# A written-out issue order for 17 tiles of a ConvFFN, with sums of block products grown in PSUM

## The chip, the cores and the metric

The kernel runs on one core of a Trainium2 chip. The metric is the device time of one execution in microseconds (us), for the whole two-layer network. TensorE (PE) multiplies, VectorE (DVE), ScalarE (ACT) and GpSimd (POOL) do the rest, and SyncE (SP) issues the DMAs.

## The reference

Two trunk layers over 1024 latent tokens and 256 context tokens of width 1024: Fourier mixing and a gating MLP in layer 0, neighbourhood attention in layer 1, and behind each a ConvFFN with 2816 inner channels. The change concerns the ConvFFN of layer 1, which has the latent tokens alone:

```python
def conv_ffn(h, w_up, conv_w, conv_b, w_down):
    L = h.shape[1]
    a = h @ w_up
    gate, val = a[..., :D_FF], a[..., D_FF:]
    gp = jnp.pad(gate, ((0, 0), (CONV_W // 2, CONV_W // 2), (0, 0)))
    g = gp[:, 0:L] * conv_w[0] + gp[:, 1:1 + L] * conv_w[1] + gp[:, 2:2 + L] * conv_w[2] + conv_b
    return (jax.nn.silu(g) * val) @ w_down
...
        x = x + g2 * conv_ffn(modulate(x, norm2_g[layer], sh2, sc2),
                              ffn_w_up[layer], ffn_conv_w[layer], ffn_conv_b[layer], ffn_w_down[layer])
```

All of it is float32. `gate` and `val` come from one matrix `w_up` of 1024 x 5632.

## The kernel before

Every float32 operand of a matmul is held as two parts, a high one (a rounded copy, written by ScalarE) and a low one (the rest, `TENSOR_TENSOR` subtract, on VectorE or GpSimd). A product of two such operands is three matmuls (`PASSES`).

The tokens of a ConvFFN are worked in two halves (`s` = 0 and 1). A half has 2 x 256 columns in the first and 2 x 258 in the second (a few overlap for the convolution). Inside a half, a loop over `f` = 0 to 21 makes one tile of 128 gate and 128 value channels at a time (`up`, L274). With the channels split in gate and value, the inner dimension in two, and the columns in two, a tile is a 2 x 2 block product, done with seven products instead of eight:

- P1 = A00 B00, P2 = A01 B10, P3 = S4 B11, P4 = A11 N4, P5 = S1 T1, P6 = S2 T2, P7 = S3 T3, where A00, A01 come from the weights of the gate channels (load 0), A10, A11 from those of the value channels (load 1), and S1 = A10 + A11, S3 = A00 - A10, S2 = S1 - A00, S4 = A01 - S2.
- c00 = P1 + P2 is the gate for the first columns, c01 the gate for the second ones, c10 and c11 the values. They need U = P1 + P6 and V = U + P7: c01 = U + P5 + P3, c11 = V + P5, c10 = V + P4.

Each product is 12 matmuls of 128x256 (128x258 in the second half) into a PSUM bank of its own (`pq`, 8 banks). VectorE adds the products up in SBUF with seven sums (`add`, L311); ScalarE copies P1. Then follow the gate (L315, ScalarE: the middle tap and the bias), two taps on VectorE (L317, L319), silu (L321), the product with the values (L361), and the high and low part of the result, `act`.

The down projection of a pair of tiles is spread over the two tiles that come later: in tile f four down products D0 to D3 (`down`, L366; 6 matmuls of 128x512 each, or 12 of 128x258), each added to the residual stream by VectorE (L382, one row per D; X0 to X3 below).

Weights for tile f+1 are prepared in tile f (`up_weights`, L222). Two loads of 512 KB go through SP into the two buffers of `wr`; GpSimd makes S1 (L241), S3 (L247), S2 (L248) and S4 (L251) out of them, S3, S2 and S4 in place of what they were made from. Each of the seven A and S matrices is then split into a high part (ScalarE, L447) and a low part (L448). In tiles with down products, GpSimd makes the low parts of A00, A01 and A11 (`POOL`), VectorE those of the four sums. `wh` and `wq` hold the parts, one buffer for each matrix. The weights of the down projection (`wrd`, 512 KB for every tile, `wd` for the parts) are split on ScalarE and VectorE (`prep`).

The order in the program is made by a scheduler that works with an estimated timeline. The code gives it only the order of the products (`ORDER`), which steps of the weights follow which product (`FEED`), and how many down products follow one (`AFTER`); sums and the tail of a tile have high priority. Engines issue in the order that results, and wait for each other by semaphores.

Of the kernel before, what the change touches and what calls it, by code (L numbers as in the profile page):

```python
# [15 lines left out]
P = 128  # L16
# [62 lines left out]
class Ffn:  # L79
# [145 lines left out]
    def up_weights(self, f, slots):  # L225
# [27 lines left out]
        steps = {x: lambda x=x: split(x) for x in ("A00", "S2", "S1", "S4", "A01", "S3", "A11")}  # L253
        steps.update(load0=lambda: load(0), load1=lambda: load(1), s=rows)
# [19 lines left out]
    def up(self, s, f, hooks, downs, prep, beside):  # L274
# [4 lines left out]
        g0 = s * NF + f  # L279
        self.busy = len(downs) > 0  # L280
        if g0 == 0:
# [18 lines left out]

        def product(p):
            wn, bn = self.PROD[p]
            o = net.t(net.ps, [P, 512], "pq" if p in ("P2", "P5") else "pq")[:, :n]
            for k in range(4):
                for i, (wp, sp) in enumerate(PASSES):
                    nc.tensor.matmul(o, w[wn][:, wp, k], self.part(s, bn, k, sp), start=(k == 0 and i == 0),  # L306
                                     stop=(k == 3 and i == 2))
            return o

        def add(o, x, y):  # L310
            nc.vector.tensor_tensor(o, x, y, ALU.add)  # L311

        def gate():
            w0, w1, w2 = (cw[:, j * NF + f:j * NF + f + 1] for j in range(3))
            nc.scalar.activation(g, C0, AF.Identity, bias=net.convb[:, layer * NF + f:layer * NF + f + 1], scale=w1)  # L315
# [5 lines left out]
            nc.scalar.activation(g, g, AF.Silu)  # L321
        x = {}
        todo = [("P1", lambda: nc.scalar.activation(c00, x["P1"], AF.Copy)),
                ("P1 P6", lambda: add(c10, x["P6"], c00)),
# [5 lines left out]
                ("P6 P5 P3", lambda: add(c01, c01, x["P3"])),  # L330
                ("P6 P5 P3 P2", gate)]
        order, feed = (self.ORDER if f else self.ORDER0, self.FEED if f >= 2 - s else (self.FEED0, self.FEED1)[f])
        cut = 3 - f if f < 2 and s == 0 else 7
        for i, p in enumerate(order):
# [18 lines left out]
            for fn in downs[:m]:  # L353
                fn()
# [12 lines left out]

    def down(self, s, j, d, blocks=None):
        nc, net = self.nc, self.net
        fs = j // 2 * 2, j // 2 * 2 + 1  # L370
        h = self.halves[s]
        for lo, m in blocks or self.blocks(s):
# [5 lines left out]
            for st, t0, num, c in h.live:  # L378
                a, b = max(lo, c), min(lo + m, c + num)
                if a < b:  # L380
                    x = self.xs[st][d][:, t0 + a - c:t0 + b - c]
                    nc.vector.scalar_tensor_tensor(x, pd[:, a - lo:b - lo], net.mod[:, self.layer, st, 5, d:d + 1], x,  # L382
                                                   ALU.mult, ALU.add)

    def run(self, hooks, beside, early, done):


        def prep(j):
# [3 lines left out]
            if j < NF:  # L392
                self.fetch(j)
        for s, norm in ((0, self.ahead()), (1, beside)):
            if s == 1:
                next(beside, None)
            ups = []
            for f in range(NF):
                ups.append(self.up(s, f, hooks, [lambda d=d, j=f - 2: self.down(s, j, j % 2 * 4 + d) for d in range(4)]
                                   if 2 <= f < NF - 1 else [], lambda f=f: prep(f),  # L400
# [1393 lines left out]
```

## Time and profile before

| | us |
|---|---|
| median of 3 runs | 2921.48 (2912.1 to 2925.05) |
| the profiled execution | 2920.99 |
| its span in the profile | 2919.1 |
| layer 1's ConvFFN in it, from its first products to the end | about 2130 to 2919 |

The span is what the profile covers; 1.9 us of the execution lie around it. "Busy" of TensorE comes from modelled ends of pipelined matmuls. The granted clock of TensorE is given as a share of full speed. Where the chain of waits is quoted, each row is a piece of work that released the next.

### The profile page before, as it was taken

Reading aid. Unit: us, or ns where it says so; the run is one execution under the profiler, and the core shown is the slowest. Engines: PE = TensorE matmul, PEld = TensorE weight load, DVE = VectorE, ACT = ScalarE, POOL = GpSimd, SP = SyncE. Lnnn points to the kernel's source line nnn. Section 1 sums busy time; section 2 is a strip of 40 time slices with the busy share of each in tenths; the row PEclk is TensorE's granted clock in tenths of the full one; section 3 lists DMA queues with packets and bytes.
Section 4 is the critical chain, followed back from the end, with each engine's and each line's share of the span. In section 5 each row is a group of like instructions: output and inputs, shape, how many; then the busy total and the mean of one; then the engine's idle time right before and its main releaser. Section 6 shows DMA issues by size and latency. Waiting matters only on the chain.

```text
span 2919.1 us, 47590 instructions
## 1 busy us (share of the span) xinstructions
PE 2772.8 (95%) x17978; PEld 2522.4 (86%) x17978; DVE 2216.9 (76%) x3748; ACT 1302.0 (45%) x2448; POOL 1267.9 (43%) x1044
## 2 busy tenths in 40 slices
PE   7999998899999999999999998999989999899998
PEld 4668877799999899999888888998778888799998
DVE  4243477999989999998767668996498777887786
ACT  4221314434444443443443336996354444444443
POOL 0600025455555755553311112443455665666663
PEclk9999999899999999999899999999989999999999
DMA  8663262322223222222052327772133323333323
GB/s 303 215 189 118 98 217 72 112 74 86 80 87 101 75 80 87 73 81 87 24 169 101 137 109 183 180 179 80 37 109 101 95 87 98 105 89 93 94 88 95
DMA packets 335886, 327.67 MB, mean 112 GB/s; under 512 B 16217, under 2 KB 264617, under 8 KB 335657
## 3 DMA queue, kind: packets, MB, share of 16 engines
q1 hardware_dynamic: 331509, 315.69, 35.9%
q0 software_dynamic: 3808, 7.87, 0.9%
q8 instruction: 143, 2.34, 0.3%
q10 hardware_dynamic: 340, 1.06, 0.1%
q14 instruction: 86, 0.70, 0.1%
HBM read 277.86 MB, written 46.71 MB: 111 GB/s over the span
## 4 chain that ended last, share of the span: by engine, by line
PE 61%; DVE 14%; DMA 7%; POOL 7%; issue 5%; ACT 5%; SPq 0%; POOLq 0%; DVEq 0%; ACTq 0%
PE pq L306 18%; PE pq L478 15%; PE pq L376 11%; PE ps L478 6%; DMA wr<-in_ffn_w_up_dram 4%; POOL ws L241 2%; DVE xl L382 2%; DVE wh L448 2%; PE pq L566 2%; POOL wh L448 2%; DVE hx L311 2%; PE ps L487 2%; ACT t L1227 1%; POOL wr L248 1%; DMA wd<-in_ada_w_dram 1%
## 5 line engine op out<-in xcount | busy, mean ns | idle before, releaser
L376 PE MATMUL pq<-act,wd 128*128 128x320 f32 (+3 forms) x3696 | 639.8, 322 | 59.3 <-DVE xl L382 24.5
L376 PEld LDWEIGHTS pq<-act,wd 128*128 128x128 f32 x3696 | 557.1, 193 | 92.0 <-DVE xl L382 28.7
L306 PE MATMUL pq<-hs,wh 128*128 128x320 f32 (+3 forms) x4128 | 607.5, 299 | 16.3 <-DVE xl L382 7.8
L306 PEld LDWEIGHTS pq<-hs,wh 128*128 128x128 f32 x4128 | 576.9, 191 | 26.4 <-DVE xl L382 11.2
L306 PE MATMUL pq<-hs,wq 128*128 128x320 f32 (+3 forms) x3144 | 469.8, 299 | 8.4 <-DVE wq L448 4.9
L478 PE MATMUL pq<-hs,wh 128*128 128x512 f32 (+3 forms) x2100 | 469.0, 358 | 3.6 <-DVE hs L724 1.9
L306 PEld LDWEIGHTS pq<-hs,wq 128*128 128x128 f32 x3144 | 442.5, 191 | 14.1 <-DVE wq L448 5.7
L478 PEld LDWEIGHTS pq<-hs,wh 128*128 128x128 f32 x2100 | 365.8, 193 | 78.0 <-issue 6.2
L241 POOL TENSOR_TENSOR ws<-wr 128x512 f32<-128x512 f32 x88 | 153.6, 1745 | 397.3 <-DMA wr<-in_ffn_w_up_dram 333.0
L447 ACT ACTIVATE wh<-wr 128x512 fp32r<-128x512 f32 (+1 forms) x223 | 161.8, 726 | 354.0 <-POOL wr L248 201.5
L382 DVE SCALAR_TENSOR_TENSOR xl<-pq,mod,xl 128x320 f32<-128x320 f32 (+5 forms) x616 | 304.1, 514 | 11.7 <-PE pq L376 11.6
L448 DVE TENSOR_TENSOR wh<-wr,wh 128x512 fp32r<-128x512 f32 (+1 forms) x147 | 166.9, 1135 | 184.8 <-ACT wh L447 184.5
L448 POOL TENSOR_TENSOR wq<-wr,wq 128x512 fp32r<-128x512 f32 x152 | 235.7, 1550 | 32.9 <-ACT wq L447 32.9
L478 PE MATMUL ps<-hs,wh 128*128 128x512 f32 x840 | 240.0, 405 | 3.6 <-ACT hs L721 1.8
L311 DVE TENSOR_TENSOR hx<-hx,pq 128x320 f32<-128x320 f32 (+3 forms) x440 | 196.1, 448 | 29.1 <-PE pq L306 21.6
L447 ACT ACTIVATE wq<-wr 128x512 fp32r<-128x512 f32 x262 | 160.0, 623 | 101.3 <-PE pq L306 73.2
L447 ACT ACTIVATE wh<-ws 128x512 fp32r<-128x512 f32 x172 | 107.5, 625 | 169.8 <-PE pq L306 115.4
L478 PEld LDWEIGHTS ps<-hs,wh 128*128 128x128 f32 x840 | 141.9, 191 | 41.6 <-issue 14.4
L251 POOL TENSOR_TENSOR ws<-wr 128x512 f32<-128x512 f32 x88 | 120.2, 1366 | 123.3 <-DVE wh L448 112.3
L999 POOL TENSOR_TENSOR hsp<-hsq,hsp 128x512 fp32r<-128x512 f32 (+1 forms) x40 | 47.1, 1185 | 265.5 <-ACT hsq L998 265.5
L1006 DVE RECIPROCAL hsq<-hsq 128x512 f32<-128x512 f32 (+1 forms) x40 | 121.1, 3030 | 52.9 <-ACT hsq L1005 52.1
L448 DVE TENSOR_TENSOR wd<-wrd,wd 128x512 fp32r<-128x512 f32 x176 | 155.5, 912 | 0.2 <-ACT wd L447 0.2
(310 smaller groups left out, 4555.5 us busy)
## 6 DMA issues: line engine op xcount, KB each, us to landing
wr<-in_ffn_w_up_dram SPq DMA_DIRECT2D x176, 512.0 KB, 4.4
wrd<-in_ffn_w_down_dram SPq DMA_DIRECT2D x88, 512.0 KB, 3.5
adaw<-in_ada_w_dram SPq DMA_DIRECT2D x128, 256.0 KB, 3.6
wd<-in_ada_w_dram SPq DMA_DIRECT2D x32, 512.0 KB, 5.1
wr<-in_odd_w_qkv_dram SPq DMA_DIRECT2D x24, 512.0 KB, 3.9
vd<-kvs SPq DMA_DIRECT2D x8, 1280.0 KB
v<-vd SPq DMA_DIRECT2D x16, 640.0 KB
kd<-kvs SPq DMA_DIRECT2D x8, 1280.0 KB, 4.6
```

Of the source, the lines that this page charges most:

```text
L241: op(raw["S1"], raw["A10"], raw["A11"], ALU.add)
L251: op(x, raw["A01"], raw["S2"], ALU.subtract)
L306: nc.tensor.matmul(o, w[wn][:, wp, k], self.part(s, bn, k, sp), start=(k == 0 and i == 0), stop=(k == 3 and i == 2))
L311: nc.vector.tensor_tensor(o, x, y, ALU.add)
L376: nc.tensor.matmul(pd, self.wds[j][i][:, wp, d % 4], self.acts[f][:, sp, lo:lo + m], start=(i == 0 and pi == 0), stop=(i == len(fs) - 1 an ...
L382: nc.vector.scalar_tensor_tensor(x, pd[:, a - lo:b - lo], net.mod[:, self.layer, st, 5, d:d + 1], x, ALU.mult, ALU.add)
L447: self.nc.scalar.activation(h, src, AF.Copy)
L448: return (e or self.nc.vector).tensor_tensor(l, src, f32(h), ALU.subtract)
L478: nc.tensor.matmul(o, w(wp, k), s(k, sp), start=(ki == 0 and pi == 0), stop=(ki == len(order) - 1 and pi == 2))
L487: nc.tensor.matmul(out, l[a], r[b], start=(first and i == 0), stop=(last and i == 2))
L566: nc.tensor.matmul(acc[32 * q:32 * q + 32, 0:256], self.sT[:, k, :], w[q // 2][:, 256 * (q % 2):256 * (q % 2) + 256], start=(k == 0), stop ...
L1006: nc.vector.reciprocal(r, r)
```

## The change

For layer 1 alone, tiles 4 to 20 of each half get an issue order that is written out as a list (`STEADY`), and the scheduler leaves PE, DVE, ACT and POOL in it; SP's issues are still placed by it. Other tiles and layer 0 keep their code. In the list P1 to P7 are products, D0 to D3 down products and X0 to X3 their additions, h and l the high and low parts, c00 to c11 with U and V the copies and sums, s the sum S1; a name with a minus belongs to the tile before.

In these tiles
- P6 grows on the PSUM bank of P1, P7 on that and P4 on that; P3 grows on the bank of P5. ScalarE copies P1, U, V and V + P4 out; VectorE is left with three sums (c00+, c11+, c01+).
- all seven low parts of the up weights are made by VectorE; GpSimd makes the four sums.
- high and low part of a matrix are separate steps. So are the two loads, the gate and its taps, and a down product and its addition. X2, X3, silu, the product with the values and the parts of `act` are issued in the next tile; the down products follow P7, P4 and P3, and the down weights are split behind P1.

```diff
@@ class Ffn
+    STEADY = ("P1", "X2-", "prep", "P2", "c00", "silu-", "mul-", "hA00", "P6", "acth-", "c00+", "actl-", "P5", "U", "hA01",
+              "lA00", "X3-", "P7", "hS1", "lS1", "D0", "V", "c11+", "lA01", "P4", "hS2", "hS3", "X0", "lS2", "D1", "c10",
+              "lS3", "load0", "hA11", "P3", "lA11", "load1", "X1", "D2", "hS4", "c01+", "gate", "lS4", "taps", "D3", "s")
+    FIRST, LAST = 4, NF - 2
@@ up_weights
-        def split(name):
+        def high(name):
+            nc.scalar.activation(slots[name][:, 0], raw[name], AF.Copy)
+
+        def low(name):
             x = raw[name]
-            net.split(slots[name][:, 0], slots[name][:, 1], x, nc.gpsimd if self.busy and name in self.POOL else None)
+            e = nc.gpsimd if self.busy and name in self.POOL else nc.vector
+            e.tensor_tensor(slots[name][:, 1], x, f32(slots[name][:, 0]), ALU.subtract)
             if name == "A00":
                 op(raw["A10"], x, raw["A10"], ALU.subtract)
                 op(x, raw["S1"], x, ALU.subtract)
...
@@ up
-        self.busy = len(downs) > 0
...
+        steady = self.layer == 1 and self.FIRST <= f <= self.LAST
+        self.busy = len(downs) > 0 and not steady
+        bank, adds = {}, {}
 
-        def product(p):
+        def product(p, onto=None):
+
             wn, bn = self.PROD[p]
-            o = net.t(net.ps, [P, 512], "pq" if p in ("P2", "P5") else "pq")[:, :n]
+            o = net.t(net.ps, [P, 512], "pq")[:, :n] if onto is None else onto
             for k in range(4):
                 for i, (wp, sp) in enumerate(PASSES):
-                    nc.tensor.matmul(o, w[wn][:, wp, k], self.part(s, bn, k, sp), start=(k == 0 and i == 0),
-                                     stop=(k == 3 and i == 2))
+                    nc.tensor.matmul(o, w[wn][:, wp, k], self.part(s, bn, k, sp),
+                                     start=(onto is None and k == 0 and i == 0), stop=(k == 3 and i == 2),
+                                     skip_group_check=onto is not None)
             return o
...
+        if steady:
+
+            onto = dict(P6="P1", P7="P6", P4="P7", P3="P5")
+            ops = {"c00": lambda: copy(c00, x["P1"]), "c00+": lambda: add(c00, c00, x["P2"]),
+                   "U": lambda: copy(c01, x["P6"]), "V": lambda: copy(c10, x["P7"]),
+                   "c11+": lambda: add(c11, c10, x["P5"]), "c10": lambda: copy(c10, x["P4"]),
+                   "c01+": lambda: add(c01, c01, x["P3"]), "gate": gate, "taps": taps, "prep": prep}
+            for tok in self.STEADY:
+                if tok in self.PROD:
+                    x[tok] = product(tok, x[onto[tok]] if tok in onto else None)
+                elif tok[0] == "D":
+                    adds["X" + tok[1]] = downs[int(tok[1])](True)
+                elif tok[-1] == "-":
+                    if tok[:-1] in before:
+                        before[tok[:-1]]()
...
+            self.before = dict(after, **adds)
+            return
...
@@ run
+                if f == Ffn.FIRST and self.layer == 1:
+                    region = self.net.tc.manual_schedule(engines={engines.PE, engines.DVE, engines.Activation, engines.Pool})
+                    region.__enter__()
+                if f == Ffn.LAST + 1 and self.layer == 1:
+                    region.__exit__(None, None, None)
```


Below are rows of the program in its order, one tile of the first half. First GpSimd, before: `wr_23812` is load 0, `wr_23840` load 1, `ws` holds S1 and then S4, `wh` and `wq` the parts.

```order
L241 TENSOR_TENSOR ws_23878<-wr_23840 128x512
L247 TENSOR_TENSOR wr_23840<-wr_23812,wr_23840 128x512
L448 TENSOR_TENSOR wh_20746<-wr_23812,wh_20746 128x512
L248 TENSOR_TENSOR wr_23812<-ws_23878,wr_23812 128x512
L448 TENSOR_TENSOR wq_20648<-wr_23812,wq_20648 128x512
L251 TENSOR_TENSOR ws_23878<-wr_23812 128x512
L448 TENSOR_TENSOR wq_20973<-wr_23840,wq_20973 128x512
```

The same in the changed kernel (loads `wr_23773` and `wr_23789`), with the first row of the next tile:

```order
L248 TENSOR_TENSOR ws_23812<-wr_23789 128x512
L258 TENSOR_TENSOR wr_23789<-wr_23773,wr_23789 128x512
L259 TENSOR_TENSOR wr_23773<-ws_23812,wr_23773 128x512
L262 TENSOR_TENSOR ws_23812<-wr_23773 128x512
L248 TENSOR_TENSOR ws_23979<-wr_23956 128x512
```

The three low parts (L448) have left GpSimd; the four sums follow each other.

ScalarE before, from the copy of P1 to the next gate:

```order
L323 ACTIVATE hx_23884<-pq_23886 128x256
L321 ACTIVATE g_23713<-g_23713 128x512
L447 ACTIVATE wq_20648<-wr_23812 128x512
L447 ACTIVATE act_23880<-g_23713 128x512
L447 ACTIVATE wh_20746<-wr_23812 128x512
L447 ACTIVATE wh_20747<-ws_23878 128x512
L447 ACTIVATE wq_20649<-wr_23840 128x512
L447 ACTIVATE wq_20973<-wr_23840 128x512
L447 ACTIVATE wh_20747<-ws_23878 128x512
L315 ACTIVATE g_23885<-hx_23884,cols_31_139,cols_175_786 128x512
```

ScalarE in the changed kernel, from the copy of P1 to the high part of A11:

```order
L332 ACTIVATE hx_23814<-pq_23816 128x256
L353 ACTIVATE g_23648<-g_23648 128x512
L251 ACTIVATE wh_20746<-wr_23773 128x512
L348 ACTIVATE act_23867<-g_23648 128x512
L332 ACTIVATE hx_23814<-pq_23816 128x256
L251 ACTIVATE wq_20648<-wr_23773 128x512
L251 ACTIVATE wh_20747<-ws_23812 128x512
L332 ACTIVATE hx_23814<-pq_23816 128x256
L251 ACTIVATE wh_20746<-wr_23773 128x512
L251 ACTIVATE wq_20649<-wr_23789 128x512
L332 ACTIVATE hx_23814<-pq_23816 128x256
L251 ACTIVATE wq_20973<-wr_23789 128x512
```

All four copies (L332) read one bank, `pq_23816`, and stand among the high parts in the places that the list gives them; the silu of the tile before (L353) now stands behind the copy of P1, and the high part of `act` (L348) ahead of U's copy.

VectorE before, from the product with the values:

```order
L361 TENSOR_TENSOR g_23885<-g_23885,hx_23884 128x512
L311 TENSOR_TENSOR hx_24056<-pq_24089,hx_24056 128x256
L448 TENSOR_TENSOR act_24052<-g_23885,act_24052 128x512
L311 TENSOR_TENSOR hx_24056<-hx_24056,pq_24072 128x256
L448 TENSOR_TENSOR wh_20746<-wr_23984,wh_20746 128x512
L311 TENSOR_TENSOR hx_24056<-pq_24114,hx_24056 128x256
L448 TENSOR_TENSOR wh_20747<-ws_24050,wh_20747 128x512
L311 TENSOR_TENSOR hx_24056<-hx_24056,pq_24138 128x256
L311 TENSOR_TENSOR hx_24056<-hx_24056,pq_24114 128x256
L448 TENSOR_TENSOR wq_20649<-wr_24012,wq_20649 128x512
L382 SCALAR_TENSOR_TENSOR xl_2932<-pq_24128,mod_127,xl_2932 128x510
L311 TENSOR_TENSOR hx_24056<-hx_24056,pq_24158 128x256
```

VectorE in the changed kernel, from the same product of the tile before:

```order
L354 TENSOR_TENSOR g_23815<-g_23815,hx_23814 128x512
L329 TENSOR_TENSOR hx_23981<-hx_23981,pq_24005 128x256
L352 TENSOR_TENSOR act_24034<-g_23815,act_24034 128x512
L256 TENSOR_TENSOR wh_20746<-wr_23940,wh_20746 128x512
L449 SCALAR_TENSOR_TENSOR xl_3793<-pq_23972,mod_127,xl_3793 128x510
L256 TENSOR_TENSOR wh_20747<-ws_23979,wh_20747 128x512
L329 TENSOR_TENSOR hx_23981<-hx_23981,pq_24038 128x256
L256 TENSOR_TENSOR wq_20648<-wr_23940,wq_20648 128x512
L449 SCALAR_TENSOR_TENSOR xl_2932<-pq_24072,mod_127,xl_2932 128x510
L256 TENSOR_TENSOR wh_20746<-wr_23940,wh_20746 128x512
L256 TENSOR_TENSOR wq_20649<-wr_23956,wq_20649 128x512
L256 TENSOR_TENSOR wq_20973<-wr_23956,wq_20973 128x512
```

Of the sums (L311 before, L329 now) two of this stretch are left, low parts (L256) of A00, A01 and A11 have come in, and the first addition of a down product there, X3, belongs to the tile before.

## Rows read from the trace of the kernel before

**Rows 1.** The page: the span, and busy time by engine (share, instructions).
```profile
span 2919.1 us, 47590 instructions
...
PE 2772.8 (95%) x17978; PEld 2522.4 (86%) x17978; DVE 2216.9 (76%) x3748; ACT 1302.0 (45%) x2448; POOL 1267.9 (43%) x1044
```
**Rows 2.** Stretches (us): length, busy time of PE, PEld, DVE, ACT, POOL; clock; DMA share, GB/s.
```profile
1090.00:1360.00 270.00, 269.87 (x1808) 267.77 (x1807) 246.93 (x422) 111.01 (x180) 148.71 (x98) 1.00 0.27 79
2190.42:2479.18 288.76, 272.95 (x1848) 251.07 (x1847) 225.10 (x360) 123.93 (x220) 175.88 (x119) 0.98 0.32 94
2576.57:2877.74 301.17, 278.01 (x2233) 274.98 (x2232) 231.47 (x427) 125.87 (x223) 195.54 (x121) 0.98 0.30 90
2376.85:2392.37 15.52, 15.52 (x110) 14.45 (x110) 12.06 (x20) 7.26 (x13) 9.39 (x7) 1.00 0.27 84
2594.41:2610.29 15.88, 15.88 (x134) 15.88 (x133) 11.95 (x22) 6.81 (x13) 9.94 (x7) 1.00 0.35 101
```
**Rows 3.** Timeline of ScalarE: gates of tiles 3 and 20, first half (start, us).
```profile
2190.42 0.82 ACT L315 ACTIVATE g<-hx,cols,cols 128x512 f32<-128x512 f32 x1 [1.38 <-DVE hx L311]
...
2479.18 0.82 ACT L315 ACTIVATE g<-hx,cols,cols 128x512 f32<-128x512 f32 x1 [1.96 <-DVE hx L311]
```
**Rows 4.** Chain of waits, one period of the first half: start, us, what.
```profile
2240.36 4.92 DMA wr<-in_ffn_w_up_dram
...
2245.41 1.33 POOL ws L241
...
2246.82 1.62 POOL wr L247
2248.45 1.70 POOL wh L448
...
2250.22 1.30 POOL wr L248
...
2251.55 0.64 ACT wh L447
...
2252.22 1.10 DVE wh L448
...
2254.41 1.29 POOL ws L251
2255.70 1.76 POOL wq L448
...
2257.48 4.62 DMA wr<-in_ffn_w_up_dram
```
**Rows 5.** Groups by line, 2200 to 2480 us: busy us, mean ns | idle before.
```profile
L382 DVE SCALAR_TENSOR_TENSOR xl<-pq,mod,xl 128x510 f32<-128x510 f32 x67 | 49.5, 740 | 0.0
L311 DVE TENSOR_TENSOR hx<-hx,pq 128x256 f32<-128x256 f32 x83 | 34.0, 410 | 0.6
...
L448 DVE TENSOR_TENSOR wh<-ws,wh 128x512 fp32r<-128x512 f32 x33 | 23.6, 715 | 0.0
...
L447 ACT ACTIVATE wh<-ws 128x512 fp32r<-128x512 f32 x33 | 20.6, 625 | 31.8 <-POOL ws L251 28.5 <-PE pq L306 2.8 <-POOL ws L241 0.5
...
L317 DVE SCALAR_TENSOR_TENSOR g<-hx,cols,g 128x511 f32<-128x511 f32 x16 | 11.9, 741 | 0.0
...
L323 ACT ACTIVATE hx<-pq 128x256 f32<-128x256 f32 x16 | 5.8, 364 | 0.0
```
**Rows 6.** Timeline, all engines, near 2331 us: start, us, engine, what.
```profile
2330.32 1.83 POOL L241 TENSOR_TENSOR ws<-wr 128x512 f32<-128x512 f32 x1 [5.04 <-DMA wr<-in_ffn_w_up_dram]
...
2330.93 0.42 DVE L311 TENSOR_TENSOR hx<-pq,hx 128x256 f32<-128x256 f32 x1
...
2331.71 0.98 DVE L448 TENSOR_TENSOR act<-g,act 128x512 fp32r<-128x512 f32 x1 [0.37 <-ACT act L447]
```
**Rows 7.** Chain of waits, a tile without waits: products (48) and one down product (6).
```profile
2376.85 5.69 PE pq L306 x48
2382.54 1.38 PE pq L376 x6
```

More of the change, by code (lines that the diff above doesn't have):

```diff
@@ L252, in split @@
                 raw["S4"] = x
-        steps = {x: lambda x=x: split(x) for x in ("A00", "S2", "S1", "S4", "A01", "S3", "A11")}
+        steps = {}
+        for x in ("A00", "S2", "S1", "S4", "A01", "S3", "A11"):
+            steps.update({"h" + x: lambda x=x: high(x), "l" + x: lambda x=x: low(x), x: lambda x=x: (high(x), low(x))})
         steps.update(load0=lambda: load(0), load1=lambda: load(1), s=rows)
@@ L311, in add, with copy, taps @@
             nc.vector.tensor_tensor(o, x, y, ALU.add)
+        def copy(o, x):
+            nc.scalar.activation(o, x, AF.Copy)
         def gate():
-            w0, w1, w2 = (cw[:, j * NF + f:j * NF + f + 1] for j in range(3))
-            nc.scalar.activation(g, C0, AF.Identity, bias=net.convb[:, layer * NF + f:layer * NF + f + 1], scale=w1)
+            nc.scalar.activation(g, C0, AF.Identity, bias=net.convb[:, layer * NF + f:layer * NF + f + 1],
+                                 scale=cw[:, NF + f:NF + f + 1])
+        def taps():
+            w0, _, w2 = (cw[:, j * NF + f:j * NF + f + 1] for j in range(3))
             for _, _, m, c in h.span:
@@ L320, in gate, with high, low @@
                                                ALU.mult, ALU.add)
-            nc.scalar.activation(g, g, AF.Silu)
-        x = {}
-        todo = [("P1", lambda: nc.scalar.activation(c00, x["P1"], AF.Copy)),
+        def high():
+            self.acts[f] = self.act()
+            nc.scalar.activation(self.acts[f][:, 0, :2 * h.n], g, AF.Copy)
+        def low():
+            a = self.acts[f]
+            self.tail = nc.vector.tensor_tensor(a[:, 1, :2 * h.n], g, f32(a[:, 0, :2 * h.n]), ALU.subtract)
+        after = {"silu": lambda: nc.scalar.activation(g, g, AF.Silu),
+                 "mul": lambda: nc.vector.tensor_tensor(g, g, C1, ALU.mult), "acth": high, "actl": low}
+        x = {}
+        before, self.before = self.before, {}
+        if steady:
[12 more added lines that the diff above has]
+                        before[tok[:-1]]()
+                elif tok[0] == "X":
+                    adds.pop(tok)()
+                elif tok in ops:
+                    ops[tok]()
+                elif tok in steps:
+                    steps[tok]()
+            self.before = dict(after, **adds)
+            return
+        for fn in before.values():
+            fn()
+        todo = [("P1", lambda: copy(c00, x["P1"])),
                 ("P1 P6", lambda: add(c10, x["P6"], c00)),
@@ L358, in up @@
                     steps[st]()
-        act = self.acts[f] = self.act()
+        if f == self.FIRST - 1 and self.layer == 1:
+            self.before = after
+            return
         with net.tc.high_priority():
-            nc.vector.tensor_tensor(g, g, C1, ALU.mult)
-            self.tail = net.split(act[:, 0, :2 * h.n], act[:, 1, :2 * h.n], g)
+            for fn in after.values():
+                fn()
     def blocks(self, s):
@@ L366, in blocks, with down @@
         return [(0, 2 * n)] if 2 * n <= 512 else [(0, n), (n, n)]
-    def down(self, s, j, d, blocks=None):
+    def down(self, s, j, d, blocks=None, later=False):
         nc, net = self.nc, self.net
@@ L371, in down @@
         h = self.halves[s]
+        out = []
         for lo, m in blocks or self.blocks(s):
@@ L393, in prep @@
                 self.fetch(j)
+        engines = mybir.EngineType
+        self.before = {}
         for s, norm in ((0, self.ahead()), (1, beside)):
@@ L398, in run @@
             for f in range(NF):
[L399 removed]
+                if f == Ffn.FIRST and self.layer == 1:
[3 more added lines that the diff above has]
+                    region.__exit__(None, None, None)
+                ups.append(self.up(s, f, hooks,
+                                   [lambda later, d=d, j=f - 2: self.down(s, j, j % 2 * 4 + d, None, later) for d in range(4)]
                                    if 2 <= f < NF - 1 else [], lambda f=f: prep(f),
```

26 lines of the change are left out of this document (16 added, 10 removed).

## The prediction

> **What bounds the kernel now.** I read the page's shares first [rows 1]. TensorE is called busy for 95% of the span, so at first sight there is little to win anywhere; but the change touches only layer 1's ConvFFN, and a share over the span says nothing of one stage. The second view is a table of stretches [rows 2]. The reader is to compare its first line with the next two. In layer 0's ConvFFN, 270 us hold 269.87 us of TensorE at clock 1.00. In layer 1 the stretch from the gate of tile 3 to the gate of tile 20 of the first half [rows 3] takes 288.76 us for 17 tiles, 16.99 each, with 272.95 us of TensorE and a mean clock of 0.98 (1.00 is the upper of two levels, 2.4 GHz). The same 17 tiles of the second half take 301.17 us, 17.72 each, with 278.01 us of TensorE, also at 0.98. The last two lines of the table are single tiles in which TensorE never waited: 15.52 us in the first half, 15.88 in the second. So TensorE loses 288.76 - 17 x 15.52 = 24.9 us in the first half and 301.17 - 17 x 15.88 = 31.2 us in the second: 56.1 us. Of these 15.8 + 23.2 = 39.0 are plain idleness, the lower clock accounts for about 0.02 x 590 = 11.8, and 5 us I can't place.
>
> What does it wait for? The chain of waits names it [rows 4]: no matmul stands in the repeating part. Load of the next weights 4.92 us, sum S1 on GpSimd 1.33, difference 1.62, low part of A00 1.70, difference 1.30, a high part on ScalarE 0.64, a low part on VectorE 1.10 (with an add and another low part behind it), last sum 1.29, low part of A11 1.76, and only then are both load buffers free and the next load starts, 17.12 us after the one before (2240.36 to 2257.48). This ring sets the period. GpSimd holds seven passes of it, one after another, and TensorE (15.5 to 15.9) waits for it. Layer 0's tiles are wider, so there the same ring is hidden under TensorE.
>
> **The change part by part.** *The ring.* GpSimd's three low parts go to VectorE; four raw sums stay. The two loads go out apart, each behind the last reader of its own buffer. What load 0 must now go round is 4.92 (load) + 0.63 + 0.72 (high and low of A00) + 1.30 (difference S2) + 0.63 + 0.72 (its parts) + 1.29 (last sum, which reads S2) = 10.2 us [rows 4, 5]. Load 1: 4.92 + 1.33 + 1.62 + 0.63 + 0.72 = 9.2 us, with A11's two parts beside or behind. Both are under 15.52, with 5 us over for waiting in their places, so the ring goes, and TensorE is next: it keeps its 84 product matmuls and its down matmuls, so its price doesn't change, 15.52 and 15.88.
>
> *Load of the others.* VectorE in the wait-free tile is busy 12.06 us [rows 2]. It loses four sums (7 to 3) at 0.41 and gains three low parts at 0.72 [rows 5]: 12.06 - 1.64 + 2.15 = 12.6 of 15.52. In the second half 11.95 gives 12.5 of 15.88. ScalarE gains three copies at 0.36: 7.26 + 1.1 = 8.4. GpSimd sheds three of seven passes and keeps four sums, 1.33 + 1.62 + 1.30 + 1.29 = 5.5 us. None exceeds TensorE; layer 0 ran TensorE without a gap beside a VectorE busy 246.93 of 270 us, 91%, against 81% here.
>
> *Sums in PSUM.* P6 now grows on P1's bank, P7 on that, P4 on that, P3 on P5's. Before, each product had its own bank and could start at once; now P6 must wait until ScalarE has copied P1, P7 until U is copied, P4 until V is, P3 until VectorE has read P5. A copy takes 0.36 us, and between any product and its continuation stands another: P2 (1.42), P5 (1.42), a down product (1.39) [rows 7]. If the copy runs at once it is hidden, with about 1 us to spare; uncovered it would cost up to 4 x 0.36 = 1.4 us a tile. What is ahead of it in ScalarE's queue decides. The page "PSUM — Partial Sum Buffer" of the Trainium skill (PSUM bank collisions raise a hardware error) says that two engines may not touch a bank at once, so these waits can't be left out; no run here shows a collision.
>
> *The written order.* On four engines each instruction now waits for the one ahead of it. The longest chain I find runs from P3's end in one tile to P7's start in the next; TensorE has 2 x 1.39 + 4 x 1.42 = 8.46 us of other work between the two. In it: high part of S4 0.63 (it waits for P3, and stands ahead of the gate), gate 0.82 [rows 3], two taps 1.48, then on VectorE one down sum 0.74 and two low parts of the down weights 1.44. Beside that, ScalarE may copy c00 only at the end of P1, 2 x 1.39 + 1.42 = 4.20 us after P3, so silu ends at 4.20 + 0.36 + 0.63 = 5.19; VectorE by the sum above is free at 5.11. Then the product with C1 0.72 (5.91), its high part 0.63 (6.54), and U's copy, which must also wait for P6, 7.04, so it ends at 7.40. P7 may start at 8.46: 1.06 us to spare. V and c10 have about as much. The down product waits for the low part behind it, 7.3, and now stands behind P7 and no longer behind P5: the idle time ahead of it goes. Queued behind the product with C1 on VectorE are c00's second sum, the activation's low part, the next weights; P2 of the next tile needs none of them soon.
>
> *What eats the spare time.* Two rows show VectorE held up by GpSimd [rows 6]: an activation's low part took 0.98 us, since it began while a GpSimd sum (2330.32 to 2332.15) ran, and ended 0.54 after that; the same kind of op takes 0.72 on average [rows 5]. A sum with one operand in PSUM, inside the same GpSimd pass, took 0.42 as ever. The Trainium skill, "SBUF — State Buffer" (Who interferes with whom), has it as a lock: a VectorE op with two SBUF inputs and a GpSimd op that reads SBUF exclude each other for the whole instruction. The trace agrees; it speaks against moving low parts to VectorE, since each new one can be blocked. By the lock at its worst, every GpSimd pass lost to VectorE, the time would be that of the second rival; by the rows of a tile that holds such blocks already, the forecast.
> Per block the price is 0 to 1.3 us (a whole GpSimd pass). Without a block the product's high part ends at 6.54; one whole block makes that 7.84, and U's copy ends at 8.20 of 8.46: nothing lost. Two make it 9.50, a stall of 1.04 us, three 10.80, a stall of 2.34. A block that falls while VectorE would wait for silu anyhow costs nothing. I take 0.2 us a tile, near the lower end because layer 0's row has no loss with seven passes beside a busier VectorE; 34 tiles make 7 us.
>
> *Edges.* At tile 4 and behind tile 20, in both halves, the order passes from the scheduler to the list and back; four finishing ops of a tile (2 x 0.63 + 2 x 0.72 = 2.7 us) move into the next. No row shows such a seam: -2.7 to +2.7 at each of four, I take +0.5 each, 2 us.
>
> **Sum.** -24.9 - 31.2 + 7 + 2 = -47 us. Against the profiled execution's 2920.99 us this is 2874 us; the median of the runs shown, 2921.48, lies 0.5 us above that execution, so nothing needs shifting. It assumes that the clock of these stretches returns to 1.00, as in layer 0 and in the wait-free tiles.
>
> **The rivals.**
> Friction: the chain is blocked twice, in bad places, in every tile, 1.04 us lost in each. Then 56.1 - 34 x 1.04 - 2 = 19 us are won: 2902. For it: 1 us is thin, and a list forgives nothing. Against it: most of VectorE's work in the chain waits for ScalarE or TensorE anyhow.
>
> VectorE becomes the bound. If all four GpSimd passes are lost to it whole, 12.6 + 4 x 1.3 = 17.8 us a tile in the first half against 16.99, and 17.7 in the second against 17.72: 17 x 0.8 = 14 us slower, 2935. Half as many would be 15.2, under TensorE. Against it: 12.06 holds such blocks already, from seven passes. No row shows every pass lost whole.
>
> Slower: the chain from P3 to P7 is blocked by three whole passes in each tile (S1's sum and the two differences, which can follow each other on GpSimd just when the taps, down parts and the product with C1 are due). 2.34 us a tile: 17.86 and 18.22, 17 x 0.87 + 17 x 0.50 = 23 us lost, 2944. It decides from a mean stall of (1.47 + 1.84) / 2 = 1.65 us a tile.
>
> The change doesn't reach the ring: SP still issues in order, and if the loads stay as late as now, the period stays 17.0 and 17.7: 2921. Against it: load 0 now waits only for sums and parts done by two thirds of a tile.
>
> **How the numbers follow.** Forecast 0.68, friction 0.16, VectorE bound 0.06, ring unchanged 0.03, slower 0.07. About 0.5% (14.6 us) is what a measurement of this kernel can tell from no change. Forecast and friction are faster: 0.84; VectorE bound and unchanged ring lie within: 0.09; slower 0.07. The low end of the range is all 56.1 us with a small gain at the seams, 2862. The high end is the friction case, 2904; what is left out is 0.16 of the rivals and a little of the friction case's far side.
>
> **What would show it.** Right: in the profile after, the two 17-tile stretches take 264 to 270 and 270 to 277 us at clock 1.00; the chain of waits there is TensorE's, no loads in it; GpSimd's wait for the load isn't followed by anyone's. VectorE is at about 12.6 us a tile, ScalarE at 8.4. Friction would show as TensorE idle ahead of the first matmul of P6, P7 or P4, ended by a ScalarE copy. The VectorE bound would show as VectorE without idle time. A chain of loads with a period of 17 us would say that the ring still stands. Wrong altogether: tiles of over 17 us in either stretch.

## The result, and the profile after

The changed kernel took 2871.75 us (median of 4 runs, 2870.85 to 2875.11), the kernel before, beside it, 2920.48 (2912.1 to 2925.05): a ratio of 0.9838, 95% interval 0.9814 to 0.9863. 2874 had been forecast. The profiled execution took 2870.85 us, 50.1 less than that of before. The page after, span and busy time by engine [rows 1 before]:

```profile
span 2869.1 us, 47270 instructions
...
PE 2752.9 (96%) x17978; PEld 2508.7 (87%) x17978; DVE 2279.5 (79%) x3714; ACT 1341.7 (47%) x2550; POOL 1101.6 (38%) x942
```

The table of stretches of the kernel after: length, busy time of PE, PEld, DVE, ACT and POOL, clock, DMA share, GB/s. First the 17 tiles of each half (A and B from here on), then eight steady tiles of A:

```profile
2182.72:2452.68 269.96, 264.49 (x1817) 244.72 (x1816) 255.28 (x343) 143.62 (x271) 99.00 (x68) 0.99 0.34 100
2548.80:2827.43 278.63, 272.44 (x2236) 270.85 (x2236) 266.14 (x410) 145.09 (x275) 103.52 (x70) 0.99 0.33 97
2326.83:2452.68 125.85, 125.09 (x867) 116.05 (x866) 120.34 (x161) 67.88 (x128) 46.43 (x32) 1.00 0.33 101
```

The gates that bound A, on ScalarE's timeline after [rows 3 before]:

```profile
2182.72 0.82 ACT L335 ACTIVATE g<-hx,cols,cols 128x512 f32<-128x512 f32 x1 [1.38 <-DVE hx L329]
...
2452.68 0.82 ACT L335 ACTIVATE g<-hx,cols,cols 128x512 f32<-128x512 f32 x1 [1.03 <-DVE hx L329]
```

Against [rows 2], A went from 288.76 to 269.96 (-18.8), B from 301.17 to 278.63 (-22.5), the stretch between them from 97.4 to 96.1, the tail behind B from 41.4 to 41.7. That is 42.3 us from the start of A to the end. The other 7.7 of the 50.0 us by which the span shrank lie ahead of A, 6.8 of them ahead of the layer's first gate, where the instructions are the same. In the 14 profiles of this case that gate came anywhere from 2129.35 to 2149.66 us, and in a repeat of the changed kernel (after_again, below) at 2145.50: so those 6.8 are chance, which happened to lie on the forecast's side. The clock ahead of the gate differs too: from 1400 to 1470 us 0.83 was granted before, 0.93 after and 0.85 in the repeat.

The new limit is in the last line of the table: VectorE is busy 120.34 of 125.85 us, 15.04 us a tile. The chain of waits after, one period, gate to gate in 15.73 us (start, us, what), where [rows 4] had loads and GpSimd and [rows 7] TensorE:

```profile
2358.28 0.83 ACT g L335
...
2359.14 0.76 DVE g L341
...
2361.33 1.20 DVE wd L526 x2
2362.53 0.61 DVE g L354
...
2363.17 0.64 ACT act L348
...
2363.83 1.00 DVE act L352
...
2368.80 0.82 DVE wq L256
...
2372.99 0.66 DVE xl L449
2373.65 0.34 DVE hx L329
...
2374.01 0.82 ACT g L335
```

VectorE is in it all along, but for one gate and one high part. In B it is less clear: there more than half of the chain's length is TensorE's. How long its operations take shows by line over the eight tiles (busy us, mean ns, idle time before and what ended it) [rows 5 before]; the first two rows are TensorE's and ScalarE's:

```profile
L323 PE MATMUL pq<-hs,wq 128*128 128x256 f32 x288 | 38.2, 281 | 0.8 <-ACT hx L332 0.7
L332 ACT ACTIVATE hx<-pq 128x256 f32<-128x256 f32 x32 | 12.2, 382 | 14.5 <-PE pq L323 14.1
L256 DVE TENSOR_TENSOR wq<-wr,wq 128x512 fp32r<-128x512 f32 x24 | 24.1, 1031 | 0.0
L449 DVE SCALAR_TENSOR_TENSOR xl<-pq,mod,xl 128x510 f32<-128x510 f32 x32 | 23.6, 739 | 0.0
L526 DVE TENSOR_TENSOR wd<-wrd,wd 128x512 fp32r<-128x512 f32 x16 | 10.3, 684 | 0.0
L329 DVE TENSOR_TENSOR hx<-hx,pq 128x256 f32<-128x256 f32 x24 | 9.8, 409 | 0.0
```

Additions (L449) and sums (L329) take what they took before, 0.739 and 0.409 us, and a copy (L332) 0.382. A low part of the up weights (L256) takes 1.03 us on average in the group shown (1.03 and 1.09 in the two others); the low parts of the down weights (L526), the same operation on the same shape, take 0.684. Where the 0.35 comes from is seen on the timeline of VectorE and GpSimd after (start, us) [rows 6 before]:

```profile
2362.50 1.78 POOL L248 TENSOR_TENSOR ws<-wr 128x512 f32<-128x512 f32 x1 [8.25 <-DMA wr<-in_ffn_w_up_dram]
2364.36 1.63 POOL L258 TENSOR_TENSOR wr<-wr,wr 128x512 f32<-128x512 f32 x1
2366.70 1.29 POOL L259 TENSOR_TENSOR wr<-ws,wr 128x512 f32<-128x512 f32 x1 [0.72 <-DVE wh L256]
2368.68 1.29 POOL L262 TENSOR_TENSOR ws<-wr 128x512 f32<-128x512 f32 x1 [0.69 <-DVE wh L256]
```
```profile
2363.83 1.00 DVE L352 TENSOR_TENSOR act<-g,act 128x512 fp32r<-128x512 f32 x1 [0.37 <-ACT act L348]
2364.76 1.78 DVE L256 TENSOR_TENSOR wh<-wr,wh 128x512 fp32r<-128x512 f32 x1
2366.46 0.74 DVE L449 SCALAR_TENSOR_TENSOR xl<-pq,mod,xl 128x510 f32<-128x510 f32 x1
2367.12 1.42 DVE L256 TENSOR_TENSOR wh<-ws,wh 128x512 fp32r<-128x512 f32 x1
...
2368.80 1.73 DVE L256 TENSOR_TENSOR wq<-wr,wq 128x512 fp32r<-128x512 f32 x1
```

Four operations with both inputs in SBUF took 1.00, 1.78, 1.42 and 1.73 us, and each ends 0.55 us after one of the GpSimd sums does (2362.50 + 1.78 = 2364.28 and 2363.83 + 1.00 = 2364.83, and so on). The addition between them, with one input in PSUM, took its usual 0.74. That is 1.00 + 1.78 + 1.42 + 1.73 - 4 x 0.68 = 3.2 us in one tile. It holds for all eight: of the 88 `TENSOR_TENSOR` operations of VectorE with both inputs in SBUF 32 began inside a GpSimd sum, and each of them ended 0.546 to 0.555 us after that sum did; the other 56 took 0.674 to 0.689 us.

### The profile page after: what moved, and what is told of

Read it like the earlier page. It is cut to its first block, busy times and chain, and to the rows that moved or that the text cites. A ratio compares the mean times of both kernels' runs of the same rounds, so it can differ in the third digit from the quotient of the medians.

```text
span 2869.1 us, 47270 instructions
## 1 busy us (share of the span) xinstructions
PE 2752.9 (96%) x17978; PEld 2508.7 (87%) x17978; DVE 2279.5 (79%) x3714; ACT 1341.7 (47%) x2550; POOL 1101.6 (38%) x942
## 3 DMA queue, kind: packets, MB, share of 16 engines
q10 hardware_dynamic: 340, 1.06, 0.1%
## 4 chain that ended last, share of the span: by engine, by line
PE 66%; DVE 20%; DMA 4%; issue 4%; ACT 3%; POOL 2%; SPq 0%; DVEq 0%; POOLq 0%; ACTq 0%
PE pq L323 20%; PE pq L556 15%; PE pq L439 12%; PE ps L556 6%; DVE xl L449 3%; DVE wh L256 3%; DVE wd L526 2%; DVE wq L256 2%; PE pq L644 2%; DVE g L354 2%; PE ps L565 2%; DVE hx L329 1%; DVE hs L526 1%; PE st L1284 1%; PE tl L1317 1%
## 5 line engine op out<-in xcount | busy, mean ns | idle before, releaser
L439 PE MATMUL pq<-act,wd 128*128 128x320 f32 (+3 forms) x3696 | 623.4, 319 | 20.3 <-ACT act L348 8.9
L439 PEld LDWEIGHTS pq<-act,wd 128*128 128x128 f32 x3696 | 549.9, 190 | 49.8 <-ACT act L348 12.6
L323 PE MATMUL pq<-hs,wq 128*128 128x320 f32 (+3 forms) x3144 | 471.2, 299 | 18.1 <-ACT hx L332 9.7
L248 POOL TENSOR_TENSOR ws<-wr 128x512 f32<-128x512 f32 x88 | 137.0, 1557 | 505.7 <-DMA wr<-in_ffn_w_up_dram 376.0
L449 DVE SCALAR_TENSOR_TENSOR xl<-pq,mod,xl 128x320 f32<-128x320 f32 (+5 forms) x616 | 303.7, 514 | 13.5 <-PE pq L439 13.1
L329 DVE TENSOR_TENSOR hx<-hx,pq 128x320 f32<-128x320 f32 (+3 forms) x372 | 168.0, 455 | 31.8 <-PE pq L323 25.3
L256 DVE TENSOR_TENSOR wq<-wr,wq 128x512 fp32r<-128x512 f32 x178 | 173.0, 986 | 15.4 <-ACT wq L251 15.3
L262 POOL TENSOR_TENSOR ws<-wr 128x512 f32<-128x512 f32 x88 | 120.9, 1373 | 118.6 <-DVE wh L256 112.7
L251 ACT ACTIVATE wh<-wr 128x512 fp32r<-128x512 f32 x172 | 107.6, 626 | 113.0 <-POOL wr L259 81.1
L526 DVE TENSOR_TENSOR wd<-wrd,wd 128x512 fp32r<-128x512 f32 x176 | 157.8, 932 | 0.6 <-ACT wd L525 0.5
L259 POOL TENSOR_TENSOR wr<-ws,wr 128x512 f32<-128x512 f32 x88 | 138.7, 1576 | 41.9 <-DVE wh L256 39.3
L256 DVE TENSOR_TENSOR wh<-ws,wh 128x512 fp32r<-128x512 f32 x172 | 149.3, 868 | 4.6 <-ACT wh L251 1.8
```

Source lines behind the costliest of these rows:

```text
L248: op(raw["S1"], raw["A10"], raw["A11"], ALU.add)
L251: nc.scalar.activation(slots[name][:, 0], raw[name], AF.Copy)
L256: e.tensor_tensor(slots[name][:, 1], x, f32(slots[name][:, 0]), ALU.subtract)
L526: return (e or self.nc.vector).tensor_tensor(l, src, f32(h), ALU.subtract)
```

## The experiments

From the start of A to the end of the span the same instructions follow in every kernel but for the edit, and chance at the layer's join is left out; this sum ("A to the end") is 728.68 us before and 686.38 after. Ratios are to the kernel before on the same chip.

**Is it GpSimd's sums?** Theory 1 says that GpSimd's passes hold VectorE, and that this sets the period. Theory 2 says that the long low parts are slow in themselves, theory 3 that the list's chain through ScalarE's copies makes the period 15.7. *sums_dve* gives them to VectorE, S1's sum behind the low part of `act`:

```diff
-        op = nc.gpsimd.tensor_tensor
+        def op(*args):
+            (nc.vector if self.steady else nc.gpsimd).tensor_tensor(*args)
```

> The four weight sums of tiles 4 to 20 go from GpSimd to VectorE (S1's sum stands behind the activation's low part of the next tile), all else as in the changed kernel. Theory 1 (VectorE sets the period: 11.8 us of its own work a tile, 3.2 us in which it is held by the four GpSimd passes, 0.7 us of waits for ScalarE): no GpSimd pass is left to hold it, four passes of 0.6 come in, 11.8 + 2.4 + 0.7 = 14.9 us, so TensorE sets the period, 15.52 and 15.88 us, about 8 us faster than the changed kernel, near 2864. Theory 2 (the long low parts are slow in themselves, not held by GpSimd): 15.0 + 2.4 + 0.7 = 18.1 us a tile, about 75 us slower than the changed kernel, near 2947. Theory 3 (the list's chain through ScalarE's copies sets the period): the sums stand beside that chain, no change within 5 us.

Measured: 2879.12 us (4 runs, 2866.5 to 2882.99), 0.9864 (0.9841 to 0.9887). A to the end took 680.05, 6.3 less than the changed kernel. The median is 2879 where 2864 was expected: it doesn't show this gain, and only the fastest of the four runs was profiled. Fourteen tiles of A:

```profile
2217.40:2434.91 217.51, 217.51 (x1514) 202.46 (x1513) 203.79 (x337) 120.93 (x224) 0.00 (x0) 1.00 0.34 102
```

TensorE has no gap left, 15.54 us a tile, while VectorE does four passes more a tile in less time (203.79 / 14 = 14.56). Theory 2 asked for 18.1 us a tile and theory 3 for no change; neither came. What it lost came at the exits, where the last tile took 17.54 (A) and 18.66 (B).

*sums3_dve* leaves S1's sum on GpSimd.

> Three of the four sums (S3, S2, S4) go to VectorE in the list's order, S1's sum stays on GpSimd. Theory 1: one holding pass is left, 11.8 + 3 x 0.6 + 0.8 + 0.7 = 15.1 us, TensorE sets the period, about 8 us faster than the changed kernel, near 2864. Theory 2: 15.0 + 1.8 + 0.7 = 17.5 us a tile, about 55 us slower, near 2927. Theory 3: no change.

2870.75 us (4 runs, 2863.58 to 2878.55), 0.9831 (0.9802 to 0.986); A 268.53, B 271.41, A to the end 680.22. Tiles took 15.7 in A, not the 15.52 that was expected; one pass a tile left on GpSimd still costs some of the gain.

*pool_memset* leaves the weight sums out in the steady tiles: GpSimd writes a constant into the same buffers, in the same places and with the same waits. Only its reading is gone.

```diff
+        def op(o, x, y, f):
+            if self.steady:
+                nc.gpsimd.memset(o, 0.5)
...
```

> In tiles 4 to 20 GpSimd writes a constant in place of each of the four sums (the sums are left out), same tiles, same order, same waits behind them. Theory 1 with the lock as the Trainium skill states it (SBUF - State Buffer, Who interferes with whom: only a GpSimd op that reads SBUF holds up a VectorE op with two SBUF inputs): VectorE's low parts all take about 0.68 us, VectorE is busy 11.8 us a tile, TensorE sets the period, near 2864. If a pass that only writes holds VectorE too, VectorE stays near 15 us and the time near 2872. Theory 2: low parts as long as before, 2872.

2865.65 us (4 runs, 2862.87 to 2867.75), 0.9813 (0.9794 to 0.9831). A 265.65, B 270.3. Its stretch of 15 tiles in A, and two groups by line in it:

```profile
2207.53:2440.60 233.07, 233.07 (x1621) 216.95 (x1620) 186.60 (x300) 127.91 (x242) 31.63 (x60) 1.00 0.34 102
```
```profile
L262 DVE TENSOR_TENSOR wq<-wr,wq 128x512 fp32r<-128x512 f32 x45 | 30.9, 687 | 6.1 <-ACT wq L257 6.1
...
L241 POOL MEMSET wr<- 128x512 f32 x30 | 15.8, 527 | 82.9 <-ACT hx L339 52.8 <-DMA wr<-in_ffn_w_up_dram 23.9 <-DVE xl L456 3.3
```

The low parts are back at 0.687 us, VectorE at 186.60 / 15 = 12.44 a tile, TensorE without a gap at 15.54. Memsets beside them hold nothing up: the 27 such VectorE operations of the stretch that overlap one took 0.684 us on average. So of the 15.04 us a tile, 2.6 were time in which GpSimd's reading passes held VectorE. (Added up one by one, its operations took 16.39 and 13.31 us a tile, 3.1 apart: neighbours overlap a little in the records, and the busy time counts that once.) "SBUF — State Buffer" of the Trainium skill (Who interferes with whom) says that a VectorE operation with two SBUF inputs contends with GpSimd instructions that read SBUF, not with those that only write; the 1.03 and 0.687 us agree with both halves of that.

*sums_mix* is sums_dve with the sums of tiles 19 and 20 of the first half left on GpSimd, against the loss at the exit; *after_again* is the changed kernel once more on the same chip.

> As the run with all four weight sums on VectorE, but tiles 19 and 20 of the first half keep them on GpSimd, so that the way out of the first half's list is near the changed kernel's. Theory 1 (VectorE, held by GpSimd, sets the period): 15.53 and 15.89 us a tile where the sums are on VectorE, from the gate of tile 3 of the first half to the end 6 to 12 us less than the changed kernel's 686.4. Without it: 686 or more.

> The changed kernel once more, beside the others on one chip. Its stretches from gate 3 to gate 20 should repeat, 270 and 279 us within 2. What comes ahead of layer 1's ConvFFN has the same instructions in the same order as before the change; if the 6.8 us by which its first gate came earlier is chance of the clock there, this run shows another figure.

2865.22 us (4 runs, 2861.75 to 2869.31), 0.9818 (0.9803 to 0.9834), against 2879.63 (2873.04 to 2883.25), 0.986 (0.9842 to 0.9877): the two ranges don't meet. The first half's exit is mended (A 264.82, the stretch behind it 96.67 against sums_dve's 99.99). A to the end is 674.55 against 685.22, 10.7 less, of the 6 to 12 expected. In after_again A took 270.48 and B 276.47.

**Which part broke the ring?** Four kernels take the parts apart. *own_banks* gives each product its bank and VectorE the seven sums again, with list and moved low parts kept (c00's second sum moves behind U, and c01's first stands ahead of P7):

```diff
-            onto = dict(P6="P1", P7="P6", P4="P7", P3="P5")
+            onto = {}
-                   "U": lambda: copy(c01, x["P6"]), "V": lambda: copy(c10, x["P7"]),
+                   "U": lambda: add(c10, x["P6"], c00), "c01": lambda: add(c01, x["P5"], c10),
+                   "V": lambda: add(c10, c10, x["P7"]),
...
```

> The list stays, but each product has a bank of its own again and VectorE makes seven sums in place of three; ScalarE copies P1 alone. Theory 1: VectorE gets four more sums of 0.34 to 0.41 us, 15.7 + 1.5 = 17.2 us a tile in the first half, 17.6 in the second, about 50 us slower than the changed kernel, near 2922. Theory 3 (waits of P6, P7, P4 for the copies cost the time): without those waits 0 to 8 us faster, 2864 to 2872.

2911.07 us (10 runs, 2902.24 to 2917.15), 0.9967 (0.9953 to 0.9982): some 40 us slower than the changed kernel, 50 expected. A takes 281.98 and B 293.02. VectorE is busy 15.4 us of a tile's 16.6 in A (262.12 / 17), and the chain of waits goes back and forth between it and TensorE.

*lows_pool* keeps the list and the sums in PSUM, and gives GpSimd its three low parts back, in one line:

```diff
-        self.busy = len(downs) > 0 and not steady
+        self.busy = len(downs) > 0
```

> The list stays, but the low parts of A00, A01 and A11 go back to GpSimd, which then makes seven passes a tile in the list's order. Theory 1: VectorE loses 3 x 0.6 us of its own work and is held by seven passes of 0.8 in place of four: 11.8 - 1.8 + 5.6 + 0.7 = 16.3 us a tile, about 15 to 20 us slower than the changed kernel. If only few low parts are left to be held, 10 + 0.7 + less than 4.8: TensorE sets the period, 6 to 8 us faster. If seven passes bring the ring of loads back: 17.1 and 17.7 us a tile, about 40 us slower.

2873.22 us (4 runs, 2872.36 to 2884.46), 0.9854 (0.9833 to 0.9875); A 273.54, B 272.26, together as long as in the changed kernel. GpSimd does seven passes a tile again (busy 182.16 in A), and nothing is lost; the 15 to 20 us that theory 1 asked for didn't come, for VectorE is busy only 223.26 / 17 = 13.1 us a tile. In A the chain of waits is one of loads and GpSimd's passes again, a load every 15.8 to 16.4 us; in B it is TensorE's. So with seven passes the ring is still there, only shorter than the 17 us of before.

*before_lows* is the kernel before with nothing but these low parts moved to VectorE.

> The kernel before with one part of the change alone: in tiles 4 to 20 of layer 1 the low parts of A00, A01 and A11 go to VectorE; the scheduler's order and the seven sums in SBUF stay. By the ring alone (4.92 + 1.33 + 1.62 + 1.30 + 0.64 + 0.72 + 0.61 + 1.29 + 0.72 = 13.2 us) TensorE would set the period: 15.6 and 16 us, near 2870. Theory 1: VectorE has 11.8 + 4 x 0.35 of its own and is held 3.2 us, 16.4 + 0.7 = 17.1 us a tile: within 15 us of the kernel before.

2911.58 us (10 runs, 2899.78 to 2915.23), 0.9969 (0.9955 to 0.9984); A 284.31, B 297.40, VectorE busy 255.86 in A, 15.05 a tile. In A TensorE now waits for the parts of `act` ahead of the down products. In B the ring still stands, with four passes on GpSimd: its chain of waits has a load in every tile, 17.1 to 17.8 us apart from the second on, and S1's sum in it is nearly three times as long as in [rows 4]:

```profile
2646.64 4.79 DMA wr<-in_ffn_w_up_dram
...
2651.56 3.83 POOL ws L241
...
2663.80 4.50 DMA wr<-in_ffn_w_up_dram
```

*list_only* is own_banks with the line of lows_pool, so the written order alone; *list_timed* is the same kernel again, timed; *before_again* is the kernel before.

> The list alone: each product has its own bank and VectorE seven sums, as in the run with own banks, and GpSimd makes the low parts of A00, A01 and A11 again. Theory 1 (VectorE's own work and what holds it set the period): against the run with own banks (281.98 and 293.02 us in the two stretches) as the run with GpSimd's low parts stands to the changed kernel, 0 to 4 us apart in each: 278 to 286 and 287 to 297 us. If the list had brought the gain by itself: under 275 and 280.

> The kernel before, profiled once more: its stretches repeat, 288.8 and 301.2 us within 2, while the first gate of layer 1's ConvFFN comes anywhere from 2133 to 2150 us if that is chance.

> The kernel list_only again (the list of issues and the earlier S2 high part, but own banks for P5, P6 and P7, seven sums of products and the three low parts on GpSimd as before), now timed. Theory 1 (the order of issue alone carries the gain; PSUM growth and the moved low parts cancel): stretch A near 269 us, B near 271 us (each within 2 us of its single look), from the start of A to the end of the span near 678 us, some 8 us less than the changed kernel's 685 to 686, and a ratio to the kernel before of 0.982 to 0.986. Theory 2 (the whole change is needed, and the single look was a lucky execution): A 278 to 286, B 287 to 297 and a ratio of 0.993 or more, near own_banks.

list_only took 2864.35 us in its one run, against 2922.96 of before_again: A 269.16, B 271.06, far under what was expected. list_timed: 2863.74 us (5 runs, 2856.96 to 2869.32), 0.983 (0.9812 to 0.9848). A and B in it:

```profile
2179.24:2447.21 267.97, 265.44 (x1832) 246.51 (x1831) 241.57 (x360) 126.72 (x220) 180.63 (x119) 0.99 0.33 101
2543.59:2814.94 271.35, 269.95 (x2240) 269.53 (x2239) 245.28 (x427) 127.16 (x223) 183.59 (x121) 1.00 0.33 100
```

The list carries the whole gain. A and B together, in us, with a second number where there are two profiles:

| A + B | low parts on GpSimd | on VectorE |
|---|---|---|
| scheduler's order (before) | 589.9, 590.8 | 581.7 |
| list, own banks | 540.2, 539.3 | 575.0 |
| list, sums in PSUM | 545.8 | 548.6, 547.0 |

The other two parts undo each other: moving the low parts costs 35 us, growing the sums in PSUM gives 27 of them back, and with the low parts on GpSimd it gives nothing (6 us more, from one profile; not followed up). In the medians, list alone and whole change aren't apart for certain: 0.983 and 0.9838 have overlapping intervals. From the start of A to the end the two profiles of the list alone, 677.64 and 675.96, lie 7.6 to 10.4 us under those of the whole change, 686.38 and 685.22.

**What in the list?** GpSimd's instructions in list_timed, one tile (start, us):

```profile
2325.94 1.30 POOL L248 TENSOR_TENSOR ws<-wr 128x512 f32<-128x512 f32 x1 [5.13 <-PE pq L323]
2327.19 1.74 POOL L256 TENSOR_TENSOR wh<-wr,wh 128x512 fp32r<-128x512 f32 x1
2328.89 1.29 POOL L258 TENSOR_TENSOR wr<-wr,wr 128x512 f32<-128x512 f32 x1
2330.27 1.62 POOL L259 TENSOR_TENSOR wr<-ws,wr 128x512 f32<-128x512 f32 x1
2331.96 1.30 POOL L262 TENSOR_TENSOR ws<-wr 128x512 f32<-128x512 f32 x1
2333.22 3.45 POOL L256 TENSOR_TENSOR wq<-wr,wq 128x512 fp32r<-128x512 f32 x2
```

All seven passes stand in one row without a gap, S4's sum (L262) directly behind S2's (L259). In [rows 4] there were 1.30 + 0.64 + 1.10 and two more VectorE operations between S2's start and S4's, the second of these the low part of S1:

```profile
2253.32 0.33 DVE hx L311
2253.66 0.61 DVE wh L448
```

S4 is written over S1, so it waits for S1's parts, and these stood on ScalarE and VectorE behind S2's, which wait for S2. The list has S1's parts right behind P7 and ahead of its down product; in list_timed the low part of S1 begins before the sum S2 does:

```profile
2329.48 1.25 DVE L256 TENSOR_TENSOR wh<-ws,wh 128x512 fp32r<-128x512 f32 x1
```

*list_s2first* undoes that alone, on ScalarE and VectorE (the low part of A01 is GpSimd's, and its own order stays):

```diff
-"P7", "hS1", "lS1", "D0", "V", "c11+", "lA01", "P4", "hS2", "hS3", "X0", "lS2", "D1",
+"P7", "D0", "V", "c11+", "P4", "hS2", "hS1", "hS3", "X0", "lS2", "lS1", "lA01", "D1",
```

> list_only with one thing undone in its list: the high and low part of S1 are issued behind those of S2, as in the kernel before, and the low part of A01 behind them. Theory 1 (the ring of GpSimd's passes got shorter from 17.1 to 15.9 us a tile because S1's parts are ahead of S2's, so that the sum S4 no longer waits for VectorE's low part of S1): S4 waits again, the ring is 17 us or more a tile, A 285 us or more, B likewise 285 or more, 30 us or more above list_only in all. Theory 2 (the place of S1's parts does not matter; it is the loads' or the relus' place in the list): A near 269 and B near 271 us, as in list_only, and no wait of GpSimd's S4 for VectorE.

2911.23 us (10 runs, 2907.44 to 2912.36), 0.9982 (0.9972 to 0.9992); A 292.66, B 293.01, A to the end 725.36 against list_timed's 675.96. Its chain of waits, one period:

```profile
2306.80 4.72 DMA wr<-in_ffn_w_up_dram
...
2311.68 1.43 POOL ws L248
2313.11 1.25 POOL wh L256
2314.37 1.27 POOL wr L258
...
2315.70 1.30 POOL wr L259
...
2317.03 0.64 ACT wh L251
...
2317.69 0.56 DVE wh L256
...
2318.30 0.69 DVE wh L256
...
2320.37 3.44 POOL wq L256 x2
2323.83 4.83 DMA wr<-in_ffn_w_up_dram
```

The ring of [rows 4] is back, 17.03 us long, with high part, low part, low part (2.0 us) between S2 and S4. The place of S1's two parts is worth 585.7 - 539.3 = 46 of the 51 us that list_timed gains in A and B. Where the ring still shows in list_timed's chain, in four tiles at the end of A, it is 15.6 to 15.9 us long: the list shortens the ring to about TensorE's own 15.52, and does not do away with it. Two kernels were not run: the one before with S1's parts alone moved ahead, and the changed one with them moved back. So it is open whether their place is enough by itself in the scheduler's order, and whether four passes a tile would need it.

## Why the prediction was right, and where its steps were not

The time, 2874 against 2871.75, and the direction were right, and so was the outline: TensorE lost its time to a ring of loads and GpSimd's passes, and the ring goes (the changed kernel's chain of waits has one load in A and none in B). Of the signs that it named for being right, A met its range (269.96 in 264 to 270, by a hair) and B missed it (278.63 against 270 to 277); the chain of waits in A's steady tiles was VectorE's and not TensorE's, and VectorE's load was 15.04 and not 12.6. The number also had luck: two parts that the prediction worked out, the moved low parts and the sums in PSUM, nearly cancel, and what carries most of the gain, the place of S1's parts in the list, it didn't name. The working had these faults.

- *The ring.* The moved low parts and the separated loads were named as what breaks it. With neither (list_timed: seven passes on GpSimd, both loads issued one right behind the other, as in the changed kernel too) A and B are shorter still; the moved low parts by themselves (before_lows) gained 8 us and left the ring standing in B. What shortens it, for 46 us in A and B, is the place of S1's parts. The chain of before showed it, S2, high part, low part, low part, S4; I counted its passes and not that wait. The 10.2 us for load 0 also left out S1's sum and S3's, which stand on GpSimd ahead of S2: 10.2 + 1.33 + 1.62 = 13.2, still under 15.52.
- *VectorE's load.* 12.6 us a tile was expected, and 15.04 measured. The counting was right: without GpSimd's reads it is 12.44 (pool_memset). What failed is the step that set "What eats the spare time" at 0.2 us a tile, as a delay on a chain with 1.06 us to spare. Held time is load first: 2.6 us a tile, on an engine with 3 to give. The rival "VectorE becomes the bound" asked for all four passes and called half as many, 15.2, "under TensorE"; but VectorE also stands still for (125.85 - 120.34) / 8 = 0.69 us a tile, so 15.04 makes 15.73, over TensorE's 15.52. That rival's mechanism was there, at half its strength.
- *Friction.* 0.2 us a tile was the size in steady tiles (15.73 against 15.52; 16.14 against 15.88), from the cause above and not from stalls on the chain from P3 to P7: the eight tiles hold one wait of TensorE for a copy, 0.7 us. With the rest, A lies 6.1 and B 8.7 us above TensorE's own time: 14.8 in place of 7 + 2. Of this 2.7 and 1.0 are the entries (first tiles 17.65 and 16.49, and 17.11), 3.1 three long tiles in B (17.64, 16.94, 16.94), whose cause is open; in after_again B has one of them. The exits cost nothing.
- *TensorE.* 15.52 and 15.88 a tile are what it takes where it never waits: pool_memset and sums_dve run at 15.54 and 15.89. Continuing a product on a bank that was copied out in between costs TensorE nothing that these rows show. The clock, assumed to return to 1.00, was 0.99 in A and B and 1.00 in the eight tiles.
- *ScalarE and GpSimd.* 8.4 and 5.5 us a tile expected, 67.88 / 8 = 8.5 and 46.43 / 8 = 5.8 measured.
- *The sum.* -47 stood against -50.0 in the spans; 42.3 belongs to the change, and the rest lies ahead of it. The repeats give 728.67 - 685.22 = 43.5. So the forecast was some 4 us too good, and chance covered it.

## What to carry to other kernels

Read a ring not only for the work in it but for the waits between its steps, and ask of each whether the data asks for it or only the order in a queue: here an in-place write waited for a read that stood behind an unrelated one. Price an operation that can be held by GpSimd at its held length, as load of its engine, before work is moved to it; in the changed kernel giving the sums to VectorE too was cheaper than sharing (14.56 us a tile against 15.04). A change of three parts is worth taking apart even when it works: here two of them cancel, and one alone does as well.

## What the runs showed of the hardware

A VectorE operation with two inputs in SBUF that begins inside a reading GpSimd pass ends 0.55 us after that pass (32 of 32 in the changed kernel's eight tiles), whatever was left of the pass. Holding goes both ways. In before_lows S1's sum on GpSimd takes 2.76 us on average over eleven tiles, against 1.53 before. GpSimd's low part of A00 took 1.29 us on average in list_s2first, where no such VectorE operation ran beside it in any of 16 tiles, and 1.72 in list_timed, where it began inside one in 15 of 16. A memset of the same 128x512 took 0.527 us and held no low part.
